# First modulation of a decoder layer: mod weights for two d tiles at once, other order, no GpSimd splits

## The chip, the cores and the metric

The kernel runs on one NeuronCore of a Trainium2 chip. The metric is the device time of one execution in microseconds. TensorE does the matmuls; VectorE, ScalarE and GpSimd (POOL in the profile) do the elementwise work; SyncE (SP) issues nearly all DMAs from one queue, in program order.

## The reference

One decoder layer on x (1024 tokens by 1024 channels), float32. What the change touches is the first block:

```
mod = silu(c) @ mod_w + mod_b            # 6 x 1024 values; sh1, sc1, g1, sh2, sc2, g2
h = rmsnorm(x, norm1_g) * (1 + sc1) + sh1
z = h @ w_in                             # q, k, v, forget logits, pool channels u
```

Behind it come forgetting attention in 8 heads, causal pooling, the output projection, a second modulated norm, a gated MLP with a causal convolution, and a last norm.

## The kernel before

Matmuls keep float32 accuracy by splitting each operand into a high part of the matmul's type and the rest, and adding hi x hi, lo x hi and hi x lo. So an operand costs a cast on ScalarE ("h", "HI") and a subtraction ("l", "LO") on VectorE or GpSimd.

**The opening.** The 8 token tiles of x are loaded, their squares summed (`norm_sq`), scaled (`norm_scale`: the even tile on VectorE, the odd one on GpSimd), transposed on TensorE (`norm_T`) and copied out of PSUM (`norm_evac`) into xT, one tile for each d tile j (128 of the 1024 channels). Warm-up matmuls (`warm`, counts in `WARM`) stand between. For each d tile the scale A and the shift H come from `c_act @ mod_w`: the mod weights of the tile, 8 k tiles of 128 x 2 x 128, are multiplied by one column of silu(c) each and summed on VectorE (`mod_dve`, tile accd, L306 and L308); two matmuls with a column of ones sum over partitions (`mod_end`, tile pm, L315); ScalarE makes A and H (L316, L318). For d tiles 0 and 1 the last two of eight k tiles go through TensorE instead (`mod_pe`, L296). `make_hT` writes HI (L327) and hf (L328) on ScalarE and LO = hf - HI (L329) on GpSimd, for most tiles.

**The stage psu.** For three 128-column blocks of `w_in` (q, k and u of the first round), `su_mm(j, ch)` adds d tile j: for each of two token halves (ch) nine matmuls 128x512 (L337): HI with suh, LO with suh, HI with sul, three blocks each. That is 144 matmuls. The weights come in two loads for each block (`su_load`, tile sur, in three buffers of the tag "wr") and are split by `su_split` (cast L164 on ScalarE, subtraction L165 on GpSimd). Behind psu TensorE makes two small transposes (pb, L468) and goes on to v (psv, L660 to L662), whose weights `wv_gen` splits (L358, L359).

**What sets the order.** TensorE's whole order is that of the code. In the opening, up to `startup.close()`, so are those of VectorE, ScalarE and GpSimd, and SP's up to `loads.close()`. Each engine works its queue from the front: an instruction that waits holds all behind it. SP's queue does the same with loads, and a load into a buffer waits until the buffer's last reader is done. Buffers come from tagged rings, such as the three of "wr".

Of the kernel before, what the change touches and what calls it, by code (L numbers as in the profile page):

```python
# [8 lines left out]
F32 = mybir.dt.float32  # L9
# [3 lines left out]
ALU = mybir.AluOpType  # L13
# [29 lines left out]
NV = 6  # L43
# [7 lines left out]
def kernel(  # L51
# [32 lines left out]
    def Tpt(name, shape=(128, 512), dt=R):  # L84
        return T("pt", list(shape), dt, name, 4)
# [7 lines left out]
    def Twr(name, shape=(128, 512), dt=F32):  # L93
        return T("wr", list(shape), dt, name, 3)
# [57 lines left out]
    su_raw = {}  # L152
    su_w = [(Tv(f"suh{i}", (128, KT, 128)), Tv(f"sul{i}", (128, KT, 128))) for i in range(3)]

    def su_load(i, hf):
        raw = su_raw[i, hf] = Twr(f"sur{i}", (128, 4, 128))
        nc.sync.dma_start(out=raw, in_=w_in[hf * 512:(hf + 1) * 512, su_cols[i]:su_cols[i] + 128]
                          .rearrange("(k p) c -> p k c", p=128))

    def su_split(i, hf, eng):  # L160
        raw = su_raw[i, hf]
        h, l = su_w[i]
        h, l = h[:, hf * 4:hf * 4 + 4, :], l[:, hf * 4:hf * 4 + 4, :]
# [127 lines left out]
    def mod_pe(j):

        pm = pms[j] = B1("pm")
        for g in range(2):
            for k in range(NV, KT):
                mm(pm[:, 0:2], lhsT=mst[j][1][:, k % 4, g, :], rhs=cact[:, k, 1 - g:3 - g],  # L296
                   start=g == 0 and k == NV, stop=False)

    def mod_dve(j, k0=0, k1=KT):
        if k0 == 0:  # L300
            accs[j] = Ts2("accd")
        acc = accs[j]
        for k in range(k0, k1):
            m = mst[j][k // 4][:, k % 4]
            if k == 0:
                nc.vector.tensor_scalar(out=acc, in0=m, scalar1=cact[:, 0, 1:2], scalar2=None, op0=ALU.mult)  # L306
            else:
                nc.vector.scalar_tensor_tensor(out=acc, in0=m, scalar=cact[:, k, 1:2], in1=acc,  # L308
                                               op0=ALU.mult, op1=ALU.add)

    def mod_end(j):
        fresh = j not in pms
        pm = B1("pm") if fresh else pms[j]
        for g in range(2):
            mm(pm[:, 0:2], lhsT=accs[j][:, g, :], rhs=one_z[:, 1 - g:3 - g], start=fresh and g == 0, stop=g == 1)  # L315
# [28 lines left out]
    def wv_gen(vh, r):  # L344
# [3 lines left out]
        for k0 in range(0, KT, g):  # L348
# [27 lines left out]
    def norm_pair(t):  # L376
        rs[t // 2] = rstd_a(sst[t // 2], "n1", 2)
# [19 lines left out]
    for g in range(4):
        norm_evac(2, g)
    warm(WARM[3])
    norm_T(4)  # L400
# [7 lines left out]
    warm(WARM[4])
    mod_pe(0)
    mod_dve(0, 4, NV)  # L410
    norm_evac(4, 2)
    norm_evac(4, 3)
    for i in range(3):
        su_split(i, 0, nc.gpsimd)
    norm_T(6, (0, 1))
    norm_evac(6, 0)
    mod_end(0)
    norm_T(6, (2, 3))
    mod_dve(1, 0, 4)
    make_hT(0, 0, nc.vector)  # L420
    for g in range(1, 4):
        norm_evac(6, g)
    su_mm(0, 0, (0,))
    mod_dve(1, 4, NV)
    mod_pe(1)
    su_mm(0, 0, (1, 2))
    make_hT(0, 1, nc.gpsimd)
    for i in range(3):
        su_load(i, 1)
    for j in range(4, KT):  # L430
        load_mod_d(j)
    load_wv(0)
    nc.sync.dma_start(out=wf_raw, in_=w_in[:, 3 * AW:3 * AW + 8].rearrange("(k p) c -> p k c", p=128))
    w0 = []
    w0g = wv_gen(0, w0)
    for j in range(KT):
        if j > 0:
            su_mm(j, 0, (0,))
        if j + 1 < KT:
            mod_end(j + 1)  # L440
            if j + 2 < KT:
                mod_dve(j + 2)
        if j > 0:
            su_mm(j, 0, (1, 2))
        if j + 1 < KT:
            eng = nc.gpsimd if j + 1 < LOJ else nc.vector
            make_hT(j + 1, 0, eng)
            make_hT(j + 1, 1, eng)
        for i in {1: (0, 1), 2: (2,)}.get(j, ()):
            su_split(i, 1, nc.gpsimd)  # L450
        if j == 6:
            next(w0g, 0)
        su_mm(j, 1)
    next(w0g, 0)
# [1308 lines left out]
```

## Time and profile before

| | |
|---|---|
| median of 3 runs | 1107.23 us (1107.12 to 1108.35) |
| profiled execution, its own time | 1108.36 us |
| span of the profile | 1106.6 us |
| TensorE busy | 1071.8 us (97%) |
| VectorE, ScalarE, GpSimd busy | 877.4, 590.8, 184.9 us |
| mean granted TensorE clock | 0.989 |

All rows are from the one profiled execution. Times of instructions are in microseconds from the start of the span. [...] Busy shares are means over all stages; the rows below are of the opening.

### The profile page before, as it was taken

What the parts mean: (1) busy time and instruction counts of PE and PEld (TensorE: products, weight loads), DVE (VectorE), ACT (ScalarE), POOL (GpSimd) and SP (SyncE); (2) the same over time, 40 slices, a digit from 0 to 9 for tenths busy, and PEclk for the clock granted to TensorE, in tenths of its full rate; (3) what the DMA queues carried; (4) which work ended last, traced back from release to release, by engine and by line L of the source; (5) the groups of instructions that cost most, each with busy time, mean ns of one, the idle gap of its engine ahead of it and who ended that gap; (6) DMA issues with size and microseconds to landing.
All of it is one profiled execution on the core that took longest, in us unless ns stands there. A gap on an engine that the chain in (4) does not pass through costs nothing.

```text
span 1106.6 us, 15492 instructions
## 1 busy us (share of the span) xinstructions
PE 1071.8 (97%) x5400; PEld 894.6 (81%) x5400; DVE 877.4 (79%) x1562; ACT 590.8 (53%) x1085; POOL 184.9 (17%) x185
## 2 busy tenths in 40 slices
PE   7899999989999999999999999999999999999997
PEld 7689887768877788888888888888888888788885
DVE  6987578878668645889877777788887869969986
ACT  7664445545667605766544545555655545425434
POOL 4565243336256510000000000000000000000000
PEclk9899999999999999999999999999999999999999
DMA  9953265371333612205322232324334289992474
GB/s 297 293 185 91 52 207 145 91 202 45 64 66 104 219 39 92 80 20 140 108 95 77 76 95 74 133 99 168 117 135 139 88 282 381 387 338 86 144 247 152
DMA packets 138389, 161.90 MB, mean 146 GB/s; under 512 B 9597, under 2 KB 94409, under 8 KB 138313
## 3 DMA queue, kind: packets, MB, share of 16 engines
q1 hardware_dynamic: 133561, 143.89, 41.8%
q10 hardware_dynamic: 4752, 17.04, 3.9%
q8 instruction: 42, 0.69, 0.3%
q14 instruction: 34, 0.28, 0.1%
HBM read 126.26 MB, written 30.45 MB: 142 GB/s over the span
## 4 chain that ended last, share of the span: by engine, by line
PE 76%; DVE 13%; DMA 4%; ACT 3%; issue 3%; POOL 0%; SPq 0%; DVEq 0%; ACTq 0%; POOLq 0%
PE ua L1297 19%; PE ub L1297 10%; PE da L1297 9%; PE db L1297 6%; PE z L923 5%; PE uc L1297 5%; DMA mrow<-in_mod_w_dram 3%; PE po L986 2%; PE po L984 2%; PE po L988 2%; PE psu L337 2%; PE pv L829 2%; DVE P L775 2%; PE psv L661 1%; PE psv L662 1%
## 5 line engine op out<-in xcount | busy, mean ns | idle before, releaser
L1262 ACT CAST uh<-wraw 128x512 fp32r<-128x512 f32 x128 | 79.2, 622 | 122.1 <-PE ua L1297 78.2
L1263 DVE TENSOR_TENSOR ul<-wraw,uh 128x512 fp32r<-128x512 f32 x128 | 87.5, 684 | 15.8 <-PE ub L1297 10.4
L1297 PE MATMUL ua<-t,uh 128*128 128x512 f32 x320 | 98.7, 390 | 0.3 <-ACT u L1341 0.3
L786 ACT ACTIVATE P<-P,mn 128x128 f32<-128x128 f32 (+3 forms) x64 | 49.7, 777 | 76.0 <-DVE mn L775 41.9
L793 POOL TENSOR_SCALAR P<-P,ri 128x128 f32<-128x128 f32 (+3 forms) x64 | 65.7, 1028 | 136.7 <-DVE ri L792 129.2
L810 DVE TENSOR_TENSOR pl<-tpp,ph 128x512 fp32r<-128x512 f32 (+1 forms) x80 | 50.7, 634 | 34.1 <-ACT ph L809 33.8
L1297 PEld LDWEIGHTS ua<-t,uh 128*128 128x128 f32 x320 | 59.9, 188 | 13.2 <-ACT u L1341 0.7
L1297 PE MATMUL da<-th,sl 128*128 128x512 f32 (+1 forms) x166 | 63.6, 383 | 1.6 <-DVE sl L1615 1.6
L775 DVE CUSTOM_DVE_ANT_0 P<-s,Fb 128x512 f32<-128x512 f32 (+2 forms) x96 | 50.2, 552 | 17.6 <-PE s L773 10.3
L1297 PE MATMUL da<-th,sh 128*128 128x512 f32 (+1 forms) x166 | 63.4, 382 | 0.5 <-DVE sv L1629 0.5
L1297 PE MATMUL da<-tl,sh 128*128 128x512 f32 (+1 forms) x166 | 63.3, 381 | 0.0
L1297 PE MATMUL ua<-t,ul 128*128 128x512 f32 x160 | 62.3, 389 | 0.0
L1297 PE MATMUL ua<-HIb,uh 128*128 128x512 f32 x160 | 62.2, 389 | 0.0
L1297 PE MATMUL ua<-LOb,uh 128*128 128x512 f32 x160 | 62.2, 389 | 0.0
L1297 PE MATMUL ua<-HIb,ul 128*128 128x512 f32 x160 | 62.2, 389 | 0.0
L923 PE MATMUL z<-HIb,wh 128*128 128x512 f32 x144 | 60.6, 421 | 0.0
L1374 DVE SCALAR_TENSOR_TENSOR tvv<-cv,colB,tvv 128x1023 f32<-128x1023 f32 (+1 forms) x44 | 56.2, 1279 | 5.2 <-ACT tvv L1372 4.8
L923 PE MATMUL z<-LOb,wh 128*128 128x512 f32 x144 | 59.4, 412 | 0.0
L923 PE MATMUL z<-HIb,wl 128*128 128x512 f32 x144 | 59.0, 409 | 0.0
L1374 DVE SCALAR_TENSOR_TENSOR tg<-cg,colB,tg 128x1023 f32<-128x1023 f32 (+1 forms) x44 | 56.3, 1279 | 1.0 <-ACT tg L1372 0.9
L809 ACT CAST ph<-tpp 128x512 fp32r<-128x512 f32 (+1 forms) x80 | 43.1, 540 | 20.5 <-PE tpp L802 9.7
L1297 PE MATMUL db<-th,sh 128*128 128x512 f32 x132 | 51.3, 389 | 0.0
(322 smaller groups left out, 3158.4 us busy)
## 6 DMA issues: line engine op xcount, KB each, us to landing
wraw<-in_ffn_up_dram SPq DMA_DIRECT2D x88, 256.0 KB, 3.4
mrow<-in_mod_w_dram SPq DMA_DIRECT2D x32, 512.0 KB, 8.3
actd<-tvv ACTq DMA_DIRECT2D x22, 512.0 KB, 2.7
ra<-in_ffn_down_dram SPq DMA_DIRECT2D x44, 256.0 KB, 5.3
x<-in_x_dram SPq DMA_DIRECT2D x16, 512.0 KB, 5.0
mst<-in_mod_w_dram SPq DMA_DIRECT2D x32, 256.0 KB, 5.4
ra<-actd SPq DMA_DIRECT2D x29, 256.0 KB, 5.7
rb<-in_ffn_down_dram SPq DMA_DIRECT2D x22, 256.0 KB, 5.2
```

Of the source, the lines that this page charges most:

```text
L337: mm(su_ps[i, ch], lhsT=su_w[i][w][:, j, :], rhs=act[j][:, ch * 512:(ch + 1) * 512], start=j == 0 and n == 0, stop=j == KT - 1 and n == 2)
L775: nc.vector.tensor_tensor_reduce(out=pt[:, n0:n1], in0=s[:, 0:n], in1=Fb[:, n0:n1], scale=1.0, scalar=3.0e38, op0=ALU.add, op1=ALU.min, ac ...
L786: nc.scalar.activation(out=pt, in_=pt, func=AF.Exp, scale=-1.0, bias=mn, accum_out=rs)
L793: nc.gpsimd.tensor_scalar(out=pt, in0=pt, scalar1=ri, scalar2=1.0, op0=ALU.mult, op1=ALU.mult)
L809: nc.scalar.copy(out=ph[:, 0:W], in_=tp[:, 0:W])
L810: nc.vector.tensor_sub(out=pl[:, 0:W], in0=tp[:, 0:W], in1=f(ph[:, 0:W]))
L829: mm(o, lhsT=V, rhs=x_[:, sl], start=b == 0 and not lo, stop=bool(lo and diag and kb == 1))
L923: mm(t[ch], lhsT=w[:, k, :], rhs=act[kk][:, ch * 512:(ch + 1) * 512], start=i == 0 and m == 0 and p0, stop=i == 1 and m == 3 and p1)
L1262: nc.scalar.copy(out=h, in_=src)
L1263: nc.vector.tensor_sub(out=l, in0=src, in1=f(h))
L1297: mm(*a, skip_group_check=True, **k)
L1374: nc.vector.scalar_tensor_tensor(out=t[:, sh:S], in0=s[:, 0:S - sh], scalar=cw_col[w][:, jj:jj + 1], in1=t[:, sh:S], op0=ALU.mult, op1=ALU ...
```

## The change

The mod weights are loaded and summed for two d tiles at a time: rows of 256 columns (1 KB) instead of 128 (512 bytes), four tiles of two k tiles each, and VectorE's operations are 128x512 instead of 128x256. The first pair's sums go wholly to TensorE (32 two-column matmuls). `su_load` takes three loads for each block (k tiles 0 to 1, 2 to 5, 6 to 7) instead of two. All LO and weight subtractions of the opening are on VectorE, and hf of d tile 0 too; the wv subtractions of the first half likewise. VectorE makes all PSUM copies of token tiles 0 and 1, three quarters of those of 2 and 3, and half of the others (before: half of the first four tiles'). Two of the five groups of warm-up matmuls (15 and 10) go. The sums of the next pair stand between the LO subtractions of the current pair, and `mod_end` of both its tiles ahead of the current pair's last nine matmuls (three for the first pair).

```
+    SUK = ((0, 2), (2, 6), (6, 8))
+    def su_load(i, n):
+        k0, k1 = SUK[n]
+        raw = su_raw[i, n] = Twr(f"sur{i}", (128, k1 - k0, 128))
...
+    def su_split(i, n):
...
         nc.scalar.copy(out=h, in_=raw)
-        eng.tensor_sub(out=l, in0=raw, in1=f(h))
+        nc.vector.tensor_sub(out=l, in0=raw, in1=f(h))
-    modv = mod_w.rearrange("(k p) (g j b) -> g j p k b", p=128, g=6, b=128)
+    modv = mod_w.rearrange("(k p) (g j b) -> g j p k b", p=128, g=6, b=256)
+    def load_mod_d(jp):
+        for q in range(4):
+            m = mst[jp, q] = (Tqk if jp < 2 else Tmx)("mst", (128, 2, 2, 256), F32)
             for g in range(2):
+                nc.sync.dma_start(out=m[:, :, g, :], in_=modv[g, jp][:, 2 * q:2 * q + 2, :])
...
     load_mod_d(0)
     for i in range(3):
         su_load(i, 0)
-    for j in range(1, 4):
-        load_mod_d(j)
+    load_mod_d(1)
+    for i in range(3):
+        su_load(i, 1)
...
+    def mod_pe(k0, k1):
+        for j in range(2):
...
+            for k in range(k0, k1):
+                for g in range(2):
+                    mm(pms[j][:, 0:2], lhsT=mst[0, k // 2][:, k % 2, g, b], rhs=cact[:, k, 1 - g:3 - g],
...
+    def make_hT(j, ch, dve=False):
...
+        if dve:
+            nc.vector.tensor_scalar(out=t, in0=raw, scalar1=A1[:, j:j + 1], scalar2=H1[:, j:j + 1],
+                                    op0=ALU.mult, op1=ALU.add)
+        else:
+            nc.scalar.activation(out=t, in_=raw, func=AF.Identity, scale=A1[:, j:j + 1], bias=H1[:, j:j + 1])
+        nc.vector.tensor_sub(out=LO[j][:, sl], in0=t, in1=f(HI[j][:, sl]))
...
-                nc.gpsimd.tensor_sub(out=ll, in0=raw, in1=f(hh))
+                (nc.vector if vh == 0 else nc.gpsimd).tensor_sub(out=ll, in0=raw, in1=f(hh))
...
     for i in range(3):
-        su_load(i, 1)
-    for j in range(4, KT):
-        load_mod_d(j)
+        su_load(i, 2)
+    load_mod_d(2)
+    load_mod_d(3)
     load_wv(0)
...
+        jp = j // 2 + 1
+        more = jp < KT // 2
+        if j % 2 == 0:
+            su_mm(j, 0)
+            make_hT(j + 1, 0)
+            if more:
+                mod_dve(jp, 0, 2)
+            else:
+                next(w0g, 0)
+            su_mm(j, 1)
+            make_hT(j + 1, 1)
+            if more:
+                mod_dve(jp, 2, 4)
+            if j == 2:
+                for i in range(3):
+                    su_split(i, 2)
+        else:
+            if more:
+                mod_dve(jp, 4, 6)
+            else:
+                next(w0g, 0)
+            su_mm(j, 0)
+            if more:
+                mod_dve(jp, 6, 8)
+                if j == 1:
+                    su_mm(j, 1, (0, 1))
+                mod_end(j + 1)
+                mod_end(j + 2)
+                make_hT(j + 1, 0)
+                if j == 1:
+                    for i in range(3):
+                        su_split(i, 1)
+            su_mm(j, 1, (2,) if j == 1 else (0, 1, 2))
+            if more:
+                make_hT(j + 1, 1)
```

SP's queue before, from the second half of the block weights on (sur are their buffers, mst those of the mod weights; in brackets the semaphores that a load waits for, DMAHW being earlier loads):

```order
L157 DMA sur0_544<-in_w_in_dram 128x4x128 [waits DMAHW7_49,Pool_49]
L157 DMA sur1_546<-in_w_in_dram 128x4x128 [waits DMAHW0_49,Pool_49]
L157 DMA sur2_548<-in_w_in_dram 128x4x128 [waits DMAHW1_49,Pool_49]
L176 DMA mst_550<-in_mod_w_dram 128x4x128 [waits DMAHW2_49,DVE_49,PE_49]
L176 DMA mst_550<-in_mod_w_dram 128x4x128 [waits DMAHW3_49]
```

The same place in the changed kernel, where mst_527 is the first load for d tiles 4 and 5:

```order
L160 DMA sur0_147<-in_w_in_dram 128x4x128 [waits DMAHW7_49,DVE_49]
L160 DMA sur1_149<-in_w_in_dram 128x4x128 [waits DMAHW0_49,DVE_49]
L160 DMA sur2_151<-in_w_in_dram 128x4x128 [waits DMAHW1_49,DVE_49]
L160 DMA sur0_521<-in_w_in_dram 128x2x128 [waits DMAHW7_49,DMAHW2_49,DVE_49]
L160 DMA sur1_523<-in_w_in_dram 128x2x128 [waits DMAHW3_49,DMAHW0_49,DVE_49]
L160 DMA sur2_525<-in_w_in_dram 128x2x128 [waits DMAHW4_49,DMAHW1_49,DVE_49]
L179 DMA mst_527<-in_mod_w_dram 128x2x256 [waits DMAHW5_49,PE_49]
```

Ahead of the mod weights there are now six block loads instead of three; the last three go into the buffers of the three ahead of them, and wait for the VectorE subtractions that read those.

VectorE's queue before, from the sums of d tile 1 (second half) to those of d tile 4:

```order
L329 TENSOR_TENSOR LOb<-hf,HIb 128x512
L308 SCALAR_TENSOR_TENSOR accd<-mst,cact,accd 128x256 x2
L306 TENSOR_SCALAR accd<-mst,cact 128x256
L308 SCALAR_TENSOR_TENSOR accd<-mst,cact,accd 128x256 x7
L306 TENSOR_SCALAR accd<-mst,cact 128x256
L308 SCALAR_TENSOR_TENSOR accd<-mst,cact,accd 128x256 x7
L306 TENSOR_SCALAR accd<-mst,cact 128x256
L308 SCALAR_TENSOR_TENSOR accd<-mst,cact,accd 128x256 x7
```

The changed kernel's, from the end of the second pair's sums to the end of the third pair's:

```order
L313 SCALAR_TENSOR_TENSOR accd<-mst,cact,accd 128x512 x6
L339 TENSOR_TENSOR LOb<-hf,HIb 128x512
L169 TENSOR_TENSOR sul_95<-sur_147,suh_94 128x512
L169 TENSOR_TENSOR sul_97<-sur_149,suh_96 128x512
L169 TENSOR_TENSOR sul_99<-sur_151,suh_98 128x512
L339 TENSOR_TENSOR LOb<-hf,HIb 128x512 x2
L311 TENSOR_SCALAR accd<-mst,cact 128x512
L313 SCALAR_TENSOR_TENSOR accd<-mst,cact,accd 128x512
L339 TENSOR_TENSOR LOb<-hf,HIb 128x512
L313 SCALAR_TENSOR_TENSOR accd<-mst,cact,accd 128x512 x2
L169 TENSOR_TENSOR sul_95<-sur_521,suh_94 128x256
L169 TENSOR_TENSOR sul_97<-sur_523,suh_96 128x256
```

The subtractions, which GpSimd had, now stand between the sums in VectorE's queue (the third small one and the last four multiply-adds of the pair follow).

## Rows read from the trace of the kernel before

**Rows 1.** Stretches in us: span, busy (count) of PE, PEld, DVE, ACT, POOL; PEclk, DMA, GB/s
```profile
20.00:27.20 7.20, 5.71 (x41) 5.02 (x39) 6.95 (x12) 5.02 (x15) 5.71 (x4) 0.75 1.12 286
27.20:46.80 19.60, 18.58 (x78) 15.39 (x78) 18.89 (x26) 15.16 (x30) 10.92 (x9) 0.83 1.18 287
46.80:50.80 4.00, 0.51 (x3) 0.08 (x1) 3.86 (x5) 0.31 (x1) 2.78 (x2) 1.00 1.15 316
50.80:57.80 7.00, 6.75 (x18) 5.53 (x19) 6.68 (x12) 3.44 (x6) 2.56 (x2) 0.51 0.74 201
...
80.00:100.00 20.00, 20.00 (x168) 20.00 (x167) 16.86 (x30) 6.66 (x20) 8.54 (x4) 1.00 0.50 138
```

**Rows 2.** TensorE in order of time: start us, us, engine, line, operation, count
```profile
18.44 1.86 PE L271 MATMUL tp<-ident,x 128*128 128x128 f32 x15 [0.60 <-POOL x L262]
...
20.69 1.00 PE L296 MATMUL pm<-cact,mst 128*128 128x2 f32 x8
...
27.27 1.63 PE L337 MATMUL psu<-HIb,suh 128*128 128x512 f32 x3
...
75.25 0.85 PE L337 MATMUL psu<-HIb,sul 128*128 128x512 f32 x3
75.93 0.25 PE L468 MATMUL pb<-ident,rowsB 100*128 100x100 f32 x1
...
78.22 0.36 PE L661 MATMUL psv<-wvl,HIb 128*128 128x264 f32 x1 [0.71 <-DVE wvl L365]
```

**Rows 3.** Order of time around 43 to 50 us, VectorE and GpSimd
```profile
43.68 1.41 DVE L308 SCALAR_TENSOR_TENSOR accd<-mst,cact,accd 128x256 f32<-128x256 f32 x1
...
45.27 2.91 POOL L329 TENSOR_TENSOR LOb<-hf,HIb 128x512 fp32r<-128x512 f32 x2 [0.47 <-ACT hf L328]
...
49.90 1.00 DVE L308 SCALAR_TENSOR_TENSOR accd<-mst,cact,accd 128x256 f32<-128x256 f32 x2
```

**Rows 4.** Order of time, the norm's operations on VectorE and GpSimd
```profile
11.96 0.75 DVE L261 TENSOR_SCALAR x<-x,n1y 128x1024 f32<-128x1024 f32 x1
...
12.63 1.41 DVE L284 COPY xT<-tp 128x256 f32<-128x256 f32 x4
...
15.86 0.17 DVE L236 RECIPROCAL n1y<-n1y 128x2 f32<-128x2 f32 x1 [0.16 <-ACT n1y L231]
...
16.64 0.75 DVE L261 TENSOR_SCALAR x<-x,n1y 128x1024 f32<-128x1024 f32 x1
...
21.44 1.62 POOL L262 TENSOR_SCALAR x<-x,n1y 128x1024 f32<-128x1024 f32 x1 [3.05 <-DMA sur<-in_w_in_dram]
```

**Rows 5.** Tiles accd, macc and LO: durations in ns min/median/max; last row a group: mean ns
```profile
L308 DVE SCALAR_TENSOR_TENSOR accd<-mst,cact,accd x52: 478/485/1601, 19.0 to 66.1; 128x256 f32<-128x256 f32 x52
L306 DVE TENSOR_SCALAR accd<-mst,cact x8: 343/348/1359, 18.6 to 60.6; 128x256 f32<-128x256 f32 x8
...
L536 DVE SCALAR_TENSOR_TENSOR macc<-mrow,cact,macc x28: 1256/1284/3204, 75.1 to 251.2; 128x1024 f32<-128x1024 f32 x28
...
L329 DVE TENSOR_TENSOR LOb<-hf,HIb 128x512 fp32r<-128x512 f32 x3 | 2.1, 690 | 3.7 <-ACT hf L328 3.7
```

**Rows 6.** ScalarE in order of time
```profile
21.33 1.72 ACT L164 CAST suh<-sur 128x512 fp32r<-128x512 f32 x3
...
33.84 0.35 ACT L316 ACTIVATE A<-pm,colA 128x1 f32<-128x1 f32 x1 [2.91 <-PE pm L315]
...
34.38 0.82 ACT L327 ACTIVATE HIb<-xT,H,A 128x512 fp32r<-128x512 f32 x1
35.10 0.80 ACT L328 ACTIVATE hf<-xT,H,A 128x512 f32<-128x512 f32 x1
```

**Rows 7.** SP's issues in time; a stretch with 1 KB rows; the page's DMA list
```profile
2.00 3.89 SPq L147 DMA_DIRECT2D x<-in_x_dram  x8
...
53.50:54.50 1.00, 1.00 (x4) 0.81 (x3) 0.93 (x3) 1.00 (x2) 0.29 (x1) 0.50 1.09 350
...
wraw<-in_ffn_up_dram SPq DMA_DIRECT2D x88, 256.0 KB, 3.4
```

More of the change, by code (lines that the diff above doesn't have):

```diff
@@ L273, with norm_evac @@
     xT = {}
-    def norm_evac(t, g):
+    def norm_evac(t, g, dve):
         for j in (2 * g, 2 * g + 1):
@@ L280, in norm_evac @@
             i_ = nps[t, g][:, (j % 2) * 256:(j % 2) * 256 + 256]
-            if g % 2 == 0 or t > 3:
+            if dve:
+                nc.vector.tensor_copy(out=o, in_=i_)
+            else:
                 nc.scalar.copy(out=o, in_=i_)
-            else:
-                nc.vector.tensor_copy(out=o, in_=i_)
     A1 = cp.tile([128, 8], F32, name="A1")
@@ L289, with mod_dve @@
     pms, accs = {}, {}
[L291 to L299, printed above, removed]
+    def mod_pe(k0, k1):
+        for j in range(2):
+            if k0 == 0:
+                pms[j] = B1("pm")
+            b = slice(j * 128, j * 128 + 128)
+            for k in range(k0, k1):
+                for g in range(2):
+                    mm(pms[j][:, 0:2], lhsT=mst[0, k // 2][:, k % 2, g, b], rhs=cact[:, k, 1 - g:3 - g],
+                       start=k == 0 and g == 0, stop=k == KT - 1 and g == 1)
+    def mod_dve(jp, k0, k1):
         if k0 == 0:
-            accs[j] = Ts2("accd")
-        acc = accs[j]
+            accs[jp] = Ts2("accd")
+        acc = accs[jp]
         for k in range(k0, k1):
-            m = mst[j][k // 4][:, k % 4]
+            m = mst[jp, k // 2][:, k % 2]
             if k == 0:
@@ L311, in mod_end @@
     def mod_end(j):
[L312 to L315, printed above, removed]
+        pm = pms[j] if j < 2 else B1("pm")
+        if j > 1:
+            b = slice((j % 2) * 128, (j % 2) * 128 + 128)
+            for g in range(2):
+                mm(pm[:, 0:2], lhsT=accs[j // 2][:, g, b], rhs=one_z[:, 1 - g:3 - g], start=g == 0, stop=g == 1)
         nc.scalar.activation(out=A1[:, j:j + 1], in_=pm[:, 1:2], func=AF.Identity, scale=n1_col[:, j:j + 1],
@@ L320, in Ts2 @@
     def Ts2(name):
-        return Tpt(name, (128, 2, 128), F32)
-    def make_hT(j, ch, eng):
+        return Tpt(name, (128, 2, 256), F32)
+    def make_hT(j, ch, dve=False):
         sl = slice(ch * 512, (ch + 1) * 512)
@@ L388 @@
     norm_scale(2)
-    for g in range(4):
-        norm_evac(0, g)
+    norm_evac(0, 0, True)
+    norm_evac(0, 1, True)
     warm(WARM[2])
-    norm_T(2)
+    norm_T(2, (0, 1))
     norm_sq(4)
@@ L395 @@
     norm_pair(4)
+    norm_evac(0, 2, True)
+    norm_evac(0, 3, True)
+    norm_T(2, (2, 3))
     norm_scale(4)
[L397 to L400, printed above, removed]
+    norm_evac(2, 0, True)
+    norm_evac(2, 1, True)
     norm_sq(6)
     norm_sq(7)
-    mod_dve(0, 0, 4)
-    norm_evac(4, 0)
-    norm_evac(4, 1)
     norm_pair(6)
+    norm_evac(2, 2, True)
+    norm_evac(2, 3, False)
     norm_scale(6)
[L408 to L412, printed above, removed]
-    for i in range(3):
[L414 to L427, printed above, removed]
+    norm_T(4)
+    mod_pe(0, 2)
+    for g in range(4):
+        norm_evac(4, g, g < 2)
+    norm_T(6)
+    for g in range(4):
+        norm_evac(6, g, g < 2)
+    mod_pe(2, 4)
+    mod_pe(4, 6)
+    mod_pe(6, 8)
+    mod_end(0)
+    make_hT(0, 0, True)
+    for i in range(3):
+        su_split(i, 0)
+    mod_end(1)
+    make_hT(0, 1, True)
     for i in range(3):
-        su_load(i, 1)
-    for j in range(4, KT):
-        load_mod_d(j)
+        su_load(i, 2)
+    load_mod_d(2)
+    load_mod_d(3)
     load_wv(0)
@@ L436 @@
     for j in range(KT):
[L437 to L454, printed above, removed]
+        jp = j // 2 + 1
[17 more added lines that the diff above has]
+                mod_dve(jp, 4, 6)
+            else:
+                next(w0g, 0)
[13 more added lines that the diff above has]
+                make_hT(j + 1, 1)
     loads.close()
```

20 lines of the change are left out of this document (5 added, 15 removed).

## The prediction, made before the changed kernel was run

> **What bounds the kernel now.** I read the table of stages first, since the change touches only the first 76 us of the span. From 80 to 100 us TensorE is busy all of the time [rows 1], and 97% of the whole span, so what the opening gains or loses passes to the end almost whole. Before that TensorE has holes: in 46.8 to 50.8 us it works 0.51 of 4 us, and in the 7 us behind it the granted clock is 0.51, half speed [rows 1]. The stage in question is the 144 matmuls psu (8 d tiles, 18 each); TensorE in order of time shows the first at 27.27 us and the end of the last at 75.93, where pb starts [rows 2]. Three of them take 0.68 us back to back (75.25 to 75.93), 0.227 each, so 144 need 32.7 us at full clock; the stage takes 48.7. The 16 us between are waits and half clock.
>
> The hole at 46.8 us is a wait for VectorE, as the instructions in order of time show: one multiply-add of the modulation sums takes 1.41 us while GpSimd runs a subtraction (43.68, beside GpSimd's two in 2.91 us at 45.27), and two take 1.00 us when GpSimd is idle (49.90) [rows 3]. The table of that tile says the same: 478 ns at the least, 1601 at the most [rows 5]. So GpSimd's subtractions stretch the sums, and the sums hold TensorE.
>
> **The change part by part.** Everything below is in us of the profiled execution.
>
> *Start.* The sums of the first pair go from VectorE to TensorE (32 matmuls of two columns), and the PSUM copies largely from ScalarE to VectorE. From VectorE's scaling of x tile 2 at 11.96 us, its queue up to the scaling of x tile 6 is: that scaling 0.75, four copies 1.41, four more 1.41, a small one 0.17, four small ones 0.78 (15.86 to 16.64), scaling 0.75, four copies 1.41, 0.17, two copies 0.71, 0.78; sum 8.3, so 20.3 us [rows 4]. GpSimd's scaling of x tile 7, 1.62 us, runs from there to 21.9 (before: 21.44 to 23.06) [rows 4]. Sixteen transposes at 1.86/15 us are 2.0 more, 23.9; the 24 two-column matmuls behind them, at 1.00/8 us, are 3.0, 26.9 [rows 2]. A and H (0.55, from 33.84 to 34.38) and HI at 0.72 (34.38 to 35.10) [rows 6] give 28.2. A cast of the new 128x256 size has no row: between half and all of the 0.57 that the 128x512 one takes (1.72 for three) [rows 6]; I take 0.33. First psu at 28.6, 1.3 later than now. The 25 warm-up matmuls that go cost nothing of themselves; their effect on the clock is a rival.
>
> *Sums of a pair.* A 128x512 multiply-add is not in the trace. Bounds: 0.485 (128x256) and 1.284 (128x1024) [rows 5]; on the line between, 0.75, which I take. The first product likewise between 0.343 and 0.75 [rows 4, 5]: 0.48. A pair is 0.48 + 7 x 0.75 = 5.7, against 2 x (0.34 + 7 x 0.50) = 7.7 alone and up to 2 x 8 x 1.4 = 22 beside GpSimd. That is the gain. Its price is that all LO subtractions (0.69 each [rows 5]) and the weight subtractions now stand in VectorE's one queue, between these sums. A 128x256 subtraction: 0.34 to 0.69, I take 0.42.
>
> [...]
>
> *Second pair (d tiles 2, 3).* ScalarE: three casts to 29.2, A and H of d tile 1 to 29.75, HI, HI, hf to 31.9. VectorE: LO to 32.6, the sums 5.7 with one more LO inside: 39.0.
>
> *Third pair, where the change loses.* The projection weights come now in three loads for each of three blocks of 128 columns, into three buffers. The last three loads stand on SP's queue ahead of the mod weights of pairs three and four, and each waits for the VectorE subtraction that frees its buffer. That subtraction stands behind A and H of d tile 2, hence behind the second pair's sums. So the third pair's eight loads begin late: 39.0, four matmuls 0.5, A H A H 1.1, HI and hf 1.44, three casts 1.71, last subtraction 0.69: 44.4. SP issues at 3.89/8 = 0.49 each [rows 7]: the third small load and the first quarter's two, 45.9. A 256 KB load on a queue that isn't full lands after 3.4 (median of 88) [rows 7]: 49.3. VectorE then does the sums 5.7, one LO 0.69 and three 128x256 subtractions 1.26 that stand among them: 57.0. The later quarters are there in time: 0.75 for 256 KB at the 350 GB/s of the stretch in which 1 KB rows ran [rows 7] (287 with 512 B rows [rows 1]), so the fourth at 53.8, needed at 55.5. TensorE has had its casts and subtractions by 44.4, does 21 matmuls (4.8) and stands from 49.2 to 57.0: 7.8 us, twice the hole of today.
>
> *The rest.* After a 4 us hole the clock was 0.51 for 7 us [rows 1]; I take the same here. 57.0, four small matmuls 1.0 at half clock, 58.0; seven us at half clock are 15 matmuls. The fourth pair's sums: A H A H 1.1, six HI and hf 4.3, LO 0.69, sums and one LO 6.4: 70.5. TensorE comes to it after 36 matmuls at 58.0 + 7 + 21 x 0.227 = 69.8, waits 0.7, and is through the four small ones at 71.0. The 45 matmuls left are 10.2, and LO of d tile 6 (71.0 + 1.1 + 1.44 + 0.69 = 74.2, wanted at 73.7) holds 0.5: 81.7, against 75.93. That is +5.8.
>
> *Behind the stage.* The first v matmuls waited 0.71 us for a subtraction at 78.22 [rows 2]; this one goes to VectorE, behind its LOs and two mod rows of up to 1.28. Between -0.7 and +1.5; I take 0, as it stays a wait on VectorE. TensorE's later order is unchanged, and the other engines' differs by a few neighbours: 0.
>
> **Sum.** 1108.36 us, the profiled execution, + 5.8 = 1114.2. It lies 1.1 above the median of the runs, 1107.23; on that, **1113.0**.
>
> **The rivals.** *Faster* (in time: 1097). The waits all hide: 28.6 + 32.7 + 1.5 for the small matmuls + 2.5 for five us at half clock = 65.3, 10.6 earlier. For it: no GpSimd beside VectorE, fewer VectorE us in all. Against it: VectorE alone has 11.0 of LO, 17.1 of sums, 4.6 of weights, about 1 of hf and 3 of mod rows and v weights from 28 us on, which ends at 65 only if it never waits, and it waits for each A and for the third pair's loads. It breaks even where the third pair's sums end 5.8 earlier, at 51.2; even without the held loads VectorE's queue (44.4, two LO that wait for hf at 46.8, 47.5, then 7.7) ends at 55.2.
>
> *Clock lost earlier* (slower still, 1116 to 1118). The granted clock fell within 20 to 27.2 us even with the warm-ups (0.75) [rows 1]; without them it may be down before the 24 small matmuls: 3.0 becomes 6.0, and the transposes ahead add up to 2.
>
> [...]
>
> *No difference* (1107.6): multiply-adds at their lower bound, 0.49, take 1.8 from each of three sums, 5.4 in all, and leave +0.4.
>
> **How the numbers follow.** Forecast, +2.5 to +8.5: 0.66. Clock lost earlier, above that: 0.17. Within 0.2% (2.2 us, what a measurement of this kernel can tell from none): 0.09. Faster: 0.08. So slower 0.83. The range: low from the lower bound of the multiply-adds and the 0.7 behind the stage, 1107.0; high from the clock rival at 1118.5.
>
> **What would show it.** In the changed profile: first psu at 28 to 30 us; multiply-adds at 0.75 with no 1.4 among them; SP's queue idle on VectorE before the last small weight loads, and the third pair's loads issued at 45 us or later, with hardly any DMA for some us before; one TensorE hole of 6 to 9 us that ends with the third pair's sums, and half clock behind it; pb at 80 to 84. I am wrong if those loads are issued before 40 us, if the hole is under 3 us, or if a 128x512 multiply-add takes nearer 0.5.

## The result, and the profile after

| | runs | median us | range | ratio to before, 95% |
|---|---|---|---|---|
| before | 4 | 1107.79 | 1107.12 to 1109.03 | |
| changed | 4 | 1119.07 | 1116.95 to 1125.20 | 1.0110 (1.0065 to 1.0154) |
| changed, a second time | 5 | 1117.28 | 1115.93 to 1118.73 | 1.0077 (1.0065 to 1.0089) |

The change makes the kernel slower, as forecast, but by 9 to 11 us and not by 5.8; the median of the first runs lies 0.6 us above the forecast range, 1107.0 to 1118.5. The profiled execution of the first runs is its slowest, 1125.20 us with a span of 1123.2. The second time gave a trace of the same code at 1117.05 us (span 1115.1). The two differ in one thing, so both are shown, as stretches like [rows 1] (start:end, span, busy of PE, PEld, DVE, ACT, POOL with counts, granted clock, DMA share, GB/s). First the execution of 1125 us:

```profile
8.20:18.40 10.20, 7.91 (x98) 7.28 (x96) 8.87 (x32) 8.48 (x20) 4.84 (x3) 1.00 1.05 383
18.40:42.30 23.90, 23.87 (x104) 22.87 (x103) 9.51 (x25) 8.74 (x21) 1.62 (x1) 0.50 0.53 156
...
60.10:66.10 6.00, 0.07 (x2) 0.06 (x1) 5.43 (x9) 0.00 (x0) 0.00 (x0) 0.72 1.07 349
66.10:73.00 6.90, 6.90 (x20) 5.78 (x21) 1.68 (x3) 5.56 (x11) 0.00 (x0) 0.50 1.11 321
```

and that of 1117 us:

```profile
7.40:27.90 20.50, 18.01 (x191) 17.23 (x189) 13.46 (x46) 11.83 (x29) 6.44 (x4) 1.00 1.04 352
27.90:34.70 6.80, 6.45 (x19) 5.26 (x19) 5.59 (x11) 5.91 (x13) 0.00 (x0) 0.50 0.47 124
34.70:51.80 17.10, 15.25 (x60) 11.21 (x58) 10.05 (x16) 9.05 (x18) 0.00 (x0) 0.90 0.35 104
51.80:57.80 6.00, 0.04 (x1) 0.00 (x0) 5.75 (x10) 0.00 (x0) 0.00 (x0) 0.78 1.06 347
57.80:65.40 7.60, 7.56 (x22) 6.33 (x23) 2.30 (x4) 6.18 (x12) 0.00 (x0) 0.50 1.13 327
65.40:83.10 17.70, 16.70 (x78) 13.39 (x77) 13.56 (x21) 11.24 (x23) 1.80 (x1) 1.00 0.67 208
83.10:89.30 6.20, 3.51 (x27) 3.09 (x25) 6.16 (x7) 3.89 (x7) 4.08 (x2) 1.00 1.03 323
89.30:96.10 6.80, 6.12 (x28) 6.15 (x29) 6.66 (x8) 1.40 (x5) 3.65 (x2) 0.50 0.23 59
```

In both stands the hole that the prediction named: 6 us in which TensorE does nothing, while VectorE is busy and the DMAs run at 347 to 349 GB/s, and half clock for 6.9 and 7.6 us behind it. In the first the clock is also down from 18.4 to 42.3 us, in the second only from 27.9 to 34.7. TensorE in order of time (as [rows 2]), first of the 1125 us, then of the 1117 us, shows what that costs (pm are the two-column matmuls, of which the profile keeps two records each: x48 are 24 matmuls):

```profile
20.70 3.41 PE L301 MATMUL pm<-cact,mst 128*128 128x2 f32 x16
23.98 3.65 PE L273 MATMUL tp<-ident,x 128*128 128x128 f32 x16
27.42 10.24 PE L301 MATMUL pm<-cact,mst 128*128 128x2 f32 x48
37.69 1.65 PE L347 MATMUL psu<-HIb,suh 128*128 128x512 f32 x3
...
66.07 1.83 PE L321 MATMUL pm<-cact,accd 128*128 128x2 f32 x8 [5.93 <-DVE accd L313]
...
91.31 0.25 PE L491 MATMUL pb<-ident,rowsB 100*128 100x100 f32 x1
```

```profile
19.59 1.84 PE L301 MATMUL pm<-cact,mst 128*128 128x2 f32 x16
21.30 1.96 PE L273 MATMUL tp<-ident,x 128*128 128x128 f32 x16
23.09 5.91 PE L301 MATMUL pm<-cact,mst 128*128 128x2 f32 x48
29.35 1.65 PE L347 MATMUL psu<-HIb,suh 128*128 128x512 f32 x3 [0.35 <-ACT suh L168]
...
57.84 1.84 PE L321 MATMUL pm<-cact,accd 128*128 128x2 f32 x8 [6.00 <-DVE accd L313]
...
83.07 0.25 PE L491 MATMUL pb<-ident,rowsB 100*128 100x100 f32 x1
...
87.27 0.39 PE L684 MATMUL psv<-wvl,HIb 128*128 128x264 f32 x1 [1.53 <-DVE wvl L375]
...
89.98 0.56 PE L683 MATMUL psv<-wvh,HIb 128*128 128x264 f32 x1 [1.84 <-DVE qb L528]
```

The first psu comes at 37.69 or 29.35, pb at 91.31 or 83.07. From there on the two run alike. How far the same matmul lies behind the kernel before, worked out from the traces (us; s is the first matmul of the attention scores, ua the first of the MLP, and the time in brackets is that of the kernel before):

```
                          1125 us       1117 us
first psu (27.27)          10.42           2.08
pb (75.93)                 15.38           7.14
first s (124.88)           20.67          12.70
first ua (504.36)          17.67           9.71
end of span (1106.6)       16.6            8.5
```

So in the execution of 1117 us 7.1 us are lost up to pb, 5.6 more in the v matmuls (from pb to the first s), and 4.2 come back later. About 3 of these come back between 223 and 236 us of the time before: there the old kernel waits 3.9 us and has half clock for 3.4; the changed one, arriving later, waits about 2 and keeps its clock (granted 1.00 from 224 to 245 us; before 0.92 from 215 to 236).

### The profile page after: what moved, and what is told of

The parts are those of the page before. It is cut to its first block, busy times and chain, and to the rows that moved or that the text cites. A ratio compares the mean times of both kernels' runs of the same rounds, so it can differ in the third digit from the quotient of the medians.

```text
span 1123.2 us, 15486 instructions
## 1 busy us (share of the span) xinstructions
PE 1084.8 (97%) x5415; PEld 907.7 (81%) x5415; DVE 867.3 (77%) x1568; ACT 585.6 (52%) x1072; POOL 153.5 (14%) x162
## 4 chain that ended last, share of the span: by engine, by line
PE 69%; DVE 16%; DMA 6%; ACT 5%; issue 4%; SPq 0%; POOL 0%; ACTq 0%; DVEq 0%; POOLq 0%
PE ua L1320 18%; PE ub L1320 9%; PE da L1320 6%; PE db L1320 5%; PE uc L1320 4%; PE z L946 4%; DMA mrow<-in_mod_w_dram 3%; PE po L1007 2%; PE po L1009 2%; PE po L1011 2%; PE pv L852 2%; DVE P L798 1%; PE tpp L829 1%; PE psv L683 1%; DVE accd L313 1%
```

## The experiments

All are edits of the changed kernel unless said otherwise. Times are medians, ratios are to runs of the kernel before on the same chip.

**1. The changed kernel again.** No edit.

> The changed kernel once more, unaltered, for a second trace and more times. The theory under test (T1, the start): the 24 two-column products of the first pair, 48 records of TensorE, took 10.24 us where the prediction had 3.0, and that makes most of the excess over the forecast. T1 says: again 10 us for this block (48 records x 0.21 at half clock), or 6 us (48 x 0.125) if the clock should hold this time, with the first psu at 37.7 or at about 31 to 33, and the time moves with it, 1125 with the one and 1117 with the other. The rival T2 (the held loads of the third pair): the same hole of about 6 us ends at the third pair's sums in both cases, and sets the time; the place of the first psu does not matter to the end by more than 2 us.

1117.28 us, 1.0077 (1.0065 to 1.0089). The block of 48 records took 5.91 us, the first psu came at 29.35 and all behind it moved with it: 8.34 us at the first psu are 8.24 at pb and 8.1 in the span. T1 holds and T2 falls: the hole is 6 us in both, so it does not absorb a later start.

**2. The warm-ups back.**

```
+    warm(WARM[3])
     norm_T(4)
+    warm(WARM[4])
     mod_pe(0, 2)
```

> The 25 warm-up matmuls that the change dropped are put back, 15 ahead of the transposes of x tiles 4 and 5, 10 behind them. T3 (the clock was lost because the warm-ups went): the granted clock stays at 1.0 through the transposes and the products; the 24 products take 6.0 us and not 10.24, the transposes 1.9 and not 3.0 to 3.6, the first psu comes at about 32, and the time falls by 5 to 6 us, to about 1113. T1 (the products are dear in themselves and the clock falls anyhow, as it fell at 23.7 us before the change with the warm-ups): the clock falls within 18 to 28 us all the same, the block stays above 8 us, and the time is within 2 us of the changed kernel's 1119, perhaps 1 us more for the warm-ups on TensorE's path.

1116.39 us, 1.0068 (1.0052 to 1.0085): not to be told from the changed kernel. In the profiled execution, 1112.65 us and the fastest of the six, the clock fell at 29.2 us instead of 27.9, the block took 5.42, the first psu came at 29.95 and pb at 84.88, so its start is not faster; what it gains, it gains in the v matmuls (see "Behind the stage" below). T3 falls for an execution that keeps its clock at the start. Whether warm-ups would spare one of 1125 stays open: no run shows it.

**3. Products left out.**

```
-    mod_pe(2, 4)
-    mod_pe(4, 6)
     mod_pe(6, 8)
```

> Leaves out two thirds of the first pair's late products: the d rows k = 2 to 5 of both d tiles, 16 of the 24 two-column matmuls (32 of 48 records), so A and H of d tiles 0 and 1 are not the reference's. T1 (the start sets the end): 32 x 0.21 = 6.8 us less at half clock, the first psu at about 31, all that follows (the second pair's sums, the small loads, the third pair) moves with it, and the end too: 5 to 7 us less, about 1113. T2 (the held loads and VectorE's queue set the end): TensorE gets to the hole earlier and waits there longer; the third pair's sums end at 64 to 66 us as now, and the time falls by under 2 us.

1113.08 us, 1.0043 (1.0030 to 1.0056), so 4.2 less. The first psu came at 26.52 (2.8 earlier), pb at 80.49 (2.6 earlier): the start passes on, but TensorE now waits 2.38 us for the second pair's sums. T1 in kind, less in size, as the block now cost 5.9 and not 10.

**4. The first pair shared.**

```
+    mod_dve(0, 2, 6)      # a pair's four middle products on VectorE
     norm_T(6)
...
-    mod_pe(2, 4)
-    mod_pe(4, 6)
     mod_pe(6, 8)          # and closing matmuls in mod_end(0), mod_end(1)
```

> The changed kernel with the first pair's sums shared: TensorE keeps the d rows k = 0, 1, 6, 7, VectorE takes k = 2 to 5 as four 128x512 operations (0.48 + 3 x 0.75 = 2.7 us) in its idle time at 23 to 28 us, and two closing matmuls follow for each d tile. Theory T1 (the late two-column products set the start): 16 matmuls less, 4.0 us at full clock, against 1 us of closing matmuls: the first psu at 27 and not 29.4, the psu stage ends 2 us earlier, and the time falls by 2 to 4 us to about 1114 (the kernel that leaves those 16 out came to 1113.1). Rival (VectorE is the bound there: its copies of x tiles 6 and 7 come later behind the four products, and the second pair's sums after them): the first psu not before 29, and the time within 1 us of 1117.3.

1113.65 us, 1.0040 (1.0024 to 1.0056), by the ratios 4 us less. The first psu came at 27.62, 1.7 earlier, but pb at 81.96, only 1.1 earlier. T1 holds for the start: VectorE had idle time for these products (in the changed kernel's execution of 1117 us it is busy 4.39 of the 10 us from 20 to 30), TensorE hardly any (busy 9.65). It does not explain the whole gain: another 2.4 us came in the v matmuls, 52.1 instead of 54.5, where VectorE's order is another (see "Behind the stage").

**5. The loads ahead.**

```
+    load_mod_d(2)
+    load_mod_d(3)
     for i in range(3):
         su_load(i, 2)
-    load_mod_d(2)
-    load_mod_d(3)
```

> The loads of the third and fourth pair's mod weights are issued ahead of the last three small weight loads, so they no longer wait for VectorE. T2 (the held loads set the end): the third pair's loads are issued before 40 us, the hole of 5.9 us at 60 to 66 us shrinks to under 2, the half clock behind it (62.8 to 73.0) goes, and the time falls by 7 to 10 us to about 1110. T1 (the loads were late, but VectorE's own queue is as late): VectorE waited only 2.06 us for these loads; without that wait the third pair's sums end 2 to 3 us earlier, at about 63.5, the hole is still over 3 us, and the time falls by 2 to 3 us to about 1116.

1112.84 us, 1.0038 (1.0026 to 1.0050), 4.4 less. The loads were issued at 32.2 us instead of 45.7, the hole shrank from 6.00 to 3.53, the third pair's sums ended 2.4 us earlier: by its marks T1, by its time between the two. Only 0.9 us of it is left at pb (the fourth pair's wait grew to 1.79); 2.7 us were gained in the v matmuls, where the half clock lasted 3.4 us and not 6.8. So the held loads cost 4 us, and something else holds the third pair: VectorE's own queue.

**6. The kernel before, its subtractions on VectorE.**

```
-        su_split(i, 0, nc.gpsimd)         (likewise su_split(i, 1), make_hT(0, 1))
+        su_split(i, 0, nc.vector)
-LOJ = 7
+LOJ = 0
```

> The kernel before the change with one part of the change alone: the subtractions of LO and of the projection weights go from GpSimd to VectorE; the sums stay one d tile wide, the loads and the order stay. Theory G (GpSimd's company was the price, so this part of the change is good and its other parts lose): no multiply-add above 0.6 us, 11 to 12 us of subtractions come to VectorE against some 15 us of stretching that go; the wait at 46.8 us and its half clock go, the psu stage falls from 48.7 to 42 to 45 us, and the time by 3 to 6 us, to 1102 to 1105. Rival (VectorE's one queue is as dear as GpSimd's company): LO now waits behind the next d tile's sums, TensorE waits 0.5 to 1.5 us at each of seven d tiles, and the time is 1107 to 1114.

1098.43 us, 0.9899 (0.9883 to 0.9915): 11 us faster, more than G said. The groups of VectorE's instructions from 24 to 66 us (busy, mean ns, idle before), of the kernel before and of this one:

```profile
L308 DVE SCALAR_TENSOR_TENSOR accd<-mst,cact,accd 128x256 f32<-128x256 f32 x47 | 35.7, 760 | 1.6
```

```profile
L308 DVE SCALAR_TENSOR_TENSOR accd<-mst,cact,accd 128x256 f32<-128x256 f32 x47 | 22.8, 485 | 1.6
L329 DVE TENSOR_TENSOR LOb<-hf,HIb 128x512 fp32r<-128x512 f32 x16 | 10.5, 685 | 3.0 <-ACT hf L328 3.0
```

13 us of VectorE's time go from the multiply-adds alone, more than the 10.5 that the 16 LO bring. VectorE idles 3.0 us for hf, no wait of TensorE in the psu stage is over 1.41 us, and pb comes at 69.93, 6.0 earlier; the rest of the gain comes behind pb. It is the one part of the change that was tried alone on the kernel before.

**7. GpSimd's part undone.** In the changed kernel the subtractions of su, of LO of d tiles 1 to 6 and of the v weights go back.

```
-        nc.vector.tensor_sub(out=LO[j][:, sl], ...)
+        (nc.gpsimd if 0 < j < LOJ else nc.vector).tensor_sub(out=LO[j][:, sl], ...)
```

> The changed kernel with the GpSimd part undone: the subtractions of the projection weights, of LO of d tiles 1 to 6 and of the v weights go back to GpSimd; all else stays changed. With the kernel before (1109), that kernel with VectorE subtracting (1098.4) and the changed one (1117.3) this fills a table of two by two. Theory W (the wide pairs, their order and their loads cost 17 to 20 us wherever the subtractions are done, GpSimd's part gains 11): GpSimd stretches 21 multiply-adds of 0.75 us towards 1.5 to 2, the third pair's sums end 5 to 9 us later than at 57.8, and the time is 1124 to 1130. Rival (in the changed order VectorE idles 14 us for hf, so what GpSimd takes off its queue is worth as much as the stretching costs): the time is within 3 us of 1117.3.

1120.26 us, 1.0103 (1.0077 to 1.0129): 3 us slower, nearer to the rival than to W, the intervals just overlap. The multiply-adds rose to 942 ns, but VectorE had idle time to spend: it still waits 12.6 us for mod weights. This run puts the v weights back too, which alone costs 0.46% (experiment 8), and experiment 6 left them on GpSimd; so the table of two by two closes with experiment 8 (1.0123), not with the changed kernel. Read so, the rest of the change costs 1.0% with GpSimd subtracting and 2.2% without: the two parts don't add, and in the changed order the step that gained 1% before gains nothing (1.0103 against 1.0123).

**8 and 9. The v weights on GpSimd; GpSimd silent.**

```
-                (nc.vector if vh == 0 else nc.gpsimd).tensor_sub(out=ll, ...)
+                nc.gpsimd.tensor_sub(out=ll, ...)        # 8; in 9 nc.vector,
-        nc.gpsimd.tensor_sub(out=l, in0=raw, in1=f(h))
+        (nc.vector if len(wseen) < 2 else nc.gpsimd).tensor_sub(...)   # 9
```

> The changed kernel with the subtractions of the v weights back on GpSimd, as before the change; the 24- and 16-column ones of the forget weights stay on VectorE. Theory V (behind the psu stage the change loses because the v weights' subtractions stand in VectorE's queue behind LO and mod rows while GpSimd stretches the small ones: 1.30 and 2.36 us where one alone takes 0.18): TensorE's two waits in the v matmuls, 1.53 and 1.84 us, and the half clock of 6.8 us behind them (3.4 us) shrink to the one of 0.7 that stood there before the change; the v stage falls from 54.5 to about 50 us and the time by 4 to 5 us, of which a wait at 240 us may take back 1 or 2: 1113 to 1115. Rival (GpSimd is slower at them, 6.5 us in all before the change, so the waits only change their name, and VectorE's small subtractions stay stretched): the v stage stays within 1.5 us of 54.5 and the time within 1.5 us of 1117.3.

> The changed kernel with GpSimd silent from 80 to 96 us: its subtractions of the second half of the v weights and of the first two unit weights go to VectorE too. Theory V, in the form that GpSimd beside VectorE is what makes VectorE late there: the 24- and 16-column subtractions take 0.18 to 0.4 us and not 1.30 and 2.36, the first unit of v weights is through by 85 us, qb about 3 us earlier or no later although VectorE has 4 us more work in all; both waits fall below 1 us, the half clock goes, and the time falls by 3 to 5 us to about 1113. Rival (VectorE's queue is simply too long there, whoever runs beside it): the added 4 us make qb later, the wait of 1.84 grows to 3 or more, and the time is 1117 to 1120.

On GpSimd: 1121.59 us, 1.0123 (1.0097 to 1.0150), 0.46% worse; TensorE waits 3.2 and 1.5 us. Theory V falls in its first form; even its rival was too kind. Silent: 1115.65 us, 1.0059 (1.0037 to 1.0082), unclear. VectorE and GpSimd in order of time, in the changed kernel (1117 us) and then VectorE with GpSimd silent:

```profile
83.04 1.30 DVE L375 TENSOR_TENSOR wvl<-wf_raw,wvh 128x24 fp32r<-128x24 f32 x1
84.86 2.36 DVE L375 TENSOR_TENSOR wvl<-wf_raw,wvh 128x16 fp32r<-128x16 f32 x1
...
81.30 3.00 POOL L910 TENSOR_TENSOR wl<-wraw,wh 128x512 fp32r<-128x512 f32 x1 [59.95 <-ACT wh L909]
84.25 2.93 POOL L369 TENSOR_TENSOR wvl<-wvr,wvh 128x1024 fp32r<-128x1024 f32 x1
90.09 1.28 POOL L910 TENSOR_TENSOR wl<-wraw,wh 128x512 fp32r<-128x512 f32 x1 [2.90 <-ACT wh L909]
```

```profile
84.31 0.17 DVE L375 TENSOR_TENSOR wvl<-wf_raw,wvh 128x24 fp32r<-128x24 f32 x1
...
85.61 0.17 DVE L375 TENSOR_TENSOR wvl<-wf_raw,wvh 128x16 fp32r<-128x16 f32 x1
```

The stretching is there: the two small subtractions end when GpSimd's do (84.34 and 84.30, 87.22 and 87.18), and take 0.17 alone. The wait on wvl goes, but that on qb is 2.1 us, as the rival has it. The v matmuls take 51.7 us (pb to first s) instead of 54.5, but pb comes 1.3 later, at 84.35; the time hardly shows it.

**10. The sums ahead.** The same arithmetic in another order.

```
+    load_mod_d(2)                  # ahead of su_load(i, 1); load_mod_d(3) ahead of su_load(i, 2)
+    mod_dve(1, 0, 5)               # ahead of mod_end(0)
...
         mod_end(ja)
         mod_end(jb)
+        mod_dve(p + 1, 3, 5)       # three more stand before mod_end
         make_hT(ja, 0)
+        mod_dve(p + 1, 5, 6)
         make_hT(ja, 1)
...
-        return Tpt(name, (128, 2, 256), F32)
+        return T("fb", [128, 2, 256], F32, name, 2)
```

> The changed kernel with another order on VectorE and SP and the same arithmetic: the third pair's loads stand ahead of the second small weight loads, the fourth's ahead of the last; five of the second pair's products are made before A of d tile 0 is there, and of each later pair three before the current pair's closing matmuls, the rest one between two LO subtractions; the sums lie in a buffer of their own. Theory O (VectorE is not short of time in the change, it stands idle for hf, 14 us in all, because the next sums stand behind LO in its queue, and 2.5 us for the held loads): with that idle time filled each pair takes TensorE 9.2 us and VectorE about 8.8, no wait for sums above 1.5 us is left, no half clock after 40 us, the psu stage ends at 66 to 71 instead of 83, and the time is 1100 to 1106. Rival (VectorE's work, some 40 us of it between 28 and 76 us, is the bound in any order): the waits spread over four pairs but their sum stays above 6 us, the stage ends after 77, and the time is above 1109.

1100.30 us, 0.9928 (0.9909 to 0.9947): 17 us below the changed kernel and 8 below the one before. Theory O holds by its marks: pb at 69.06, the longest wait in the psu stage 0.47, no half clock in it behind 34.9 (3 us of it come in the v matmuls, at 76 us). What VectorE waited for in the stage, in the changed kernel (1117 us) and here (us, times, longest):

```profile
DVE LOb L339 <- ACT hf L338: 13.9, 9, 4.0
DVE hf L335 <- ACT H L324: 4.8, 1, 4.8
DVE accd L311 <- DMA mst<-in_mod_w_dram: 2.5, 1, 2.5
```

```profile
DVE LOb L340 <- ACT hf L339: 5.1, 2, 4.3
```

and the stretch of this kernel that answers to the hole:

```profile
35.00:69.00 34.00, 33.53 (x157) 27.10 (x156) 28.27 (x44) 27.34 (x53) 2.52 (x1) 1.00 0.83 255
```

**11. The sums ahead, the loads held.**

```
-    load_mod_d(2)                  # back behind su_load(i, 2), with load_mod_d(3)
     su_split(i, 1)
     mod_dve(2, 0, 3)               # now in this order
```

> The kernel with the sums ahead (1100.3), but with SP's order as the change has it: the last three small weight loads again ahead of the third and fourth pair's loads, and VectorE's subtractions for the second small loads one place earlier so that they don't wait behind sums that need those loads. It parts what the order on VectorE and what the held loads cost. Theory O+Q (both cost, and in this order the held loads cost more than the 4.4 us they cost in the change, as the waiting sums stand ahead of LO): the third pair's loads are issued at 38 to 40 us and land from 43, the first sums and behind them LO of d tile 2 come at 45 to 47, TensorE, wanting that LO at about 41, waits 4 to 6 us and pays half clock behind it: 1105 to 1109. Rival (the order on VectorE alone makes the gain, the loads' place is worth nothing then): no wait above 1.5 us, within 1.5 us of 1100.3.

1109.05 us, 1.0013 (0.9992 to 1.0034), 0.8% above 10. O+Q holds, a little beyond its bounds: loads issued at 38.2, first sum at 42.62 after 4.9 us of waiting, LO of d tile 2 at 47.52, TensorE waits 6.4 for it.

```profile
42.62 0.49 DVE L311 TENSOR_SCALAR accd<-mst,cact 128x512 f32<-128x512 f32 x1 [4.90 <-DMA mst<-in_mod_w_dram]
...
48.26 1.65 PE L347 MATMUL psu<-LOb,suh 128*128 128x512 f32 x3 [6.35 <-DVE LOb L339]
```

Both the order on VectorE and that on SP are needed. The buffer of its own that the sums have in 10 and 11 was not tried apart; in the changed kernel no wait of VectorE or ScalarE from 28 to 84 us is for the old one.

**12. Both starts and the silence together.** Edits 4 and 9 on top of 10; the second pair's products follow A again.

```
+    mod_dve(0, 2, 6)
-    mod_dve(1, 0, 5)
...
+    mod_dve(1, 0, 4)
     make_hT(1, 0)
```

> The kernel with the sums ahead, with two more edits that were tried alone: VectorE takes the products k = 2 to 5 of the first pair (in place of five of the second pair's, which now follow A), and GpSimd is silent from 65 to 80 us (its subtractions for the second half of the v weights and for two unit weights go to VectorE). If the gains add (3.6 us from the start alone, 1.7 from the silence): the first psu at 27 to 28 and not 29.8, no wait above 1.5 us in the psu stage, one wait below 1.5 us in the v stage and no half clock there, 1095 to 1097. Rival (VectorE, now with 2.7 us of products more and the second pair's sums later, becomes the bound in the first 40 us, TensorE waits 1.5 to 3 us at the second pair's closing matmuls and the clock falls behind it): 1099 to 1102.

1099.38 us, 0.9925 (0.9899 to 0.9951), the same as 10: the rival. The first psu came at 27.93, but TensorE waits 0.40 us for the second pair's sums and 1.84 for an LO, with half clock for 3.4 us behind, and pb is at 71.82, 2.8 later than in 10. The v matmuls, with GpSimd silent, give that back: 49.2 us instead of 52.4.

## Why the prediction was wrong in size

The median came out 6.1 us above the forecast. 2.7 of this is the sum itself: the span grew by 8.5 us where the prediction has +5.8. Of these 1.4 came in the stage and 1.4 behind it, from the term that it put at 0. Another 2.2 are the executions of 1121 and 1125 us among the first four runs, and 1.1 the step from the profiled 1108.36 down to the median 1107.23, which the later medians of the kernel before, 1107.8 to 1109.5, don't bear out.

*Hole, right.* In the execution of 1117 us the steps came as worked out: third pair's loads issued at 45.67 (forecast 45.9), first sum at 50.25 (49.3), TensorE free at 57.84 (57.0), hole 6.0 (7.8), half clock for 7.6 us behind it (7), pb at 83.07 (81.7). One row was misread on the way, without harm: the multiply-add of 1.41 us at 43.68 ended before the two LO at 45.27 began; it ran beside two weight subtractions of GpSimd (2.76 us from 42.05).

```profile
30.31 15.27 SPq L160 DMA_DIRECT2D sur<-in_w_in_dram  x6
45.67 9.73 SPq L179 DMA_DIRECT2D mst<-in_mod_w_dram  x16
...
50.25 0.49 DVE L311 TENSOR_SCALAR accd<-mst,cact 128x512 f32<-128x512 f32 x1 [2.49 <-DMA mst<-in_mod_w_dram]
...
L313 DVE SCALAR_TENSOR_TENSOR accd<-mst,cact,accd 128x512 f32<-128x512 f32 x21 | 15.8, 751 | 0.6
```

SP's row of six loads lasts 15.27 us because the last three wait in it (in experiment 5 the first three stand alone and take 1.47). The 128x512 multiply-add takes 751 ns, as read off the line between the rows. All 21 take 743 to 753. No run of the changed kernel shows the +2.5 at the lower end of the forecast's chance; its span came out 8.5 and 16.6 longer. The remark that VectorE's queue would end at 55.2 even without the held loads was right too (experiment 5: 55.46), but not followed up: it says that without the held loads the order on VectorE still loses. By the ratios the loads alone give back 0.4% (experiment 5), the order alone 0.6% (experiment 11), and both 1.5% or 17 us (experiment 10).

*Start, right by luck.* "[T]he 24 two-column matmuls behind them, at 1.00/8 us, are 3.0": the step failed. The 8 of [rows 2] are records, two for each float32 matmul; 24 matmuls are 48 records and took 5.91. It didn't show because two other steps erred the other way. The forecast set GpSimd's scaling of x tile 7 behind VectorE's of tile 6, where the two ran side by side: the transposes began at 21.30, not after 21.9, and the products 0.8 earlier than forecast. And it set A, H, HI and the cast, 1.7 us, behind all the products, where A of d tile 0 was made at 27.66 while those of d tile 1 still ran: the first psu came 0.35 behind the last product. 2.9 - 0.8 - 1.3 leaves 0.8, and the first psu at 29.35 is within 0.75 of the forecast.

```profile
19.61 0.75 DVE L263 TENSOR_SCALAR x<-x,n1y 128x1024 f32<-128x1024 f32 x1
19.73 1.61 POOL L264 TENSOR_SCALAR x<-x,n1y 128x1024 f32<-128x1024 f32 x1 [1.89 <-issue]
...
27.66 0.35 ACT L322 ACTIVATE A<-pm,colA 128x1 f32<-128x1 f32 x1 [3.60 <-PE pm L301]
```

*Clock lost earlier.* This rival, given 0.17, came true in the profiled execution, and more dearly than priced: the clock fell at 18.4, with the transposes and the products behind it at 3.65 and 10.24 against 1.96 and 5.91, and 8.3 us at the first psu. It is not the usual case: the second set lies at 1115.9 to 1118.7, and in none of the eleven later traces of the changed kernel and its edits does the first psu come after 30.2. The runs at 1121 and 1125 lift the median of the first four by 2 us; the one at 1121 left no trace. No run can say whether the warm-ups that went would have kept the clock, since experiment 2 met no such execution. That TensorE was busy did not by itself bring the clock back: it was so for 23.87 of those 23.90 us at half clock. The clock rose at 42.3, during the 128x512 matmuls that follow. Why the same code starts either way stays open.

*Behind the stage.* "Between -0.7 and +1.5; I take 0", and "the other engines' differs by a few neighbours: 0": this is the step that failed. In the two traces of the changed kernel the v matmuls lost 5.3 and 5.6 us. TensorE's waits there, 1.53 and 1.84 instead of 0.71, are 2.7 of the 5.6, and the clock that then fell for 6.8 us is the rest. The prediction counted VectorE's own work there, and priced no clock behind so short a wait. Two more things it missed. GpSimd's weight subtractions, which the change leaves in place from 81 us on, stretch two of VectorE's small subtractions beside them (1.30 and 2.36 us, 0.17 without them); without them the v matmuls took 2.8 us less (experiment 9). And one of the few neighbours counts. Before, VectorE copies colB (from pb) out of PSUM ahead of qa and qb (from psu); in the changed kernel it comes behind them, and TensorE's second wait ends with qb. The kernel of experiment 4 happens to have the old order, with the small subtractions as long as in the changed one. VectorE before, in the changed kernel (1117 us), and VectorE and TensorE in experiment 4:

```profile
78.09 0.34 DVE L470 COPY colB<-pb 128x188 f32<-128x188 f32 x1
79.16 0.69 DVE L505 SCALAR_TENSOR_TENSOR qb<-psu,qb 64x512 fp32r<-64x512 f32 x1
```

```profile
89.14 0.69 DVE L528 SCALAR_TENSOR_TENSOR qb<-psu,qb 64x512 fp32r<-64x512 f32 x1
89.87 0.35 DVE L493 COPY colB<-pb 128x188 f32<-128x188 f32 x1
```

```profile
87.22 0.34 DVE L491 COPY colB<-pb 128x188 f32<-128x188 f32 x1
88.29 0.69 DVE L526 SCALAR_TENSOR_TENSOR qb<-psu,qb 64x512 fp32r<-64x512 f32 x1
...
87.61 0.39 PE L681 MATMUL psv<-wvh,HIb 128*128 128x264 f32 x1 [0.59 <-DVE colB L491]
```

There the second wait is 0.59 and the v matmuls take 52.1 us. The trace of experiment 2 has the old order too; TensorE, which comes 1.8 us later to pb, waits 0.58 in all, keeps its clock (1.00 from 80 to 110 us) and takes 49.1 us, as before the change (48.95). So the term is no fixed price: it hangs on when TensorE arrives and on that order. No run sets the order alone. That 4.2 us come back later the prediction did not see either: 5.6 - 4.2 is the 1.4 that, with 1.4 more in the stage, makes that span 8.5 longer and not 5.8.

*Faster.* This rival had 0.08, for "no GpSimd beside VectorE". Experiment 6 shows that this part alone is worth 11 us; with all the rest of the change on top of it the kernel is 20 us slower.

## What to carry to other kernels

Count records against instructions before dividing a duration: each two-column float32 matmul here is two (48 for 24), while the transposes (64 for 64) and the 128x512 matmuls of psu (144 for 144) are one. When work moves to an in-order engine, list where that engine now stands waiting and put the next stage's independent work there; here 13.9 us of waiting for hf fell to 5.1, and with the loads ahead the loss of 0.8% became a gain of 0.7%. Test the parts of a combined change alone: here one part was worth 1% and the whole cost 0.8%. Even reordered, the wide kernel (0.9928, and 0.9925 in experiment 12) did not come out below that part alone (0.9899). The intervals overlap; no run shows a gain from the wide sums themselves.

## What the hardware showed that was not expected

- Two small VectorE subtractions that began after one of GpSimd's ended with it: the 128x24 took 1.30 us (83.04 to 84.34, GpSimd's to 84.30), the 128x16, begun 0.6 us after GpSimd's of 2.93, took 2.36 (to 87.22, GpSimd's to 87.18); with GpSimd silent each takes 0.17. It is not so for all: a 128x512 one at 84.26, 0.01 after GpSimd's, took 0.68. Multiply-adds took 760 ns on average with GpSimd subtracting and 485 without (experiment 6). GpSimd pays as well: its 128x512 subtraction took 3.00 us when it began inside a VectorE multiply-add (81.30), and 1.28 when none ran at its start (90.09).
- At half clock the 48 records took 1.73 times as long (10.24 against 5.91), the 16 transposes 1.86 times.
- Two short waits, 1.5 and 1.8 us within 4.5 us, were followed by half clock for 6.8 us, about as much as followed the 6 us holes (6.9 and 7.6).
